# Encoder step: the background of the gated delta rule in another order

## The chip, the cores and the metric

The kernel runs on one core of one Trainium2 chip. A core has five engines that run side by side, each with its own instruction stream, taken strictly in order: TensorE (PE, matrix products; its weight loads are listed as PEld), VectorE (DVE), ScalarE (ACT), GpSimd (POOL) and SyncE (SP), which here issues the DMAs. The metric is the device time of one call in microseconds; the median of the runs is what counts.

## The reference, cut to what matters

One layer of a hybrid encoder is computed for 1024 prompt tokens and 32 sample tokens of width 1024. One large projection of the normalised input feeds four branches: A (short convolution), B (gated recurrence), C (a 31-tap convolution, then a layer norm) and D (gated delta rule with 8 heads). Their outputs are projected, gated, added, projected once more, and normalised. The parts that matter here are branch D, and the convolution of branch C:

```python
qkv, new_conv_d = causal_dwconv(col(OFF_D, 2 * W_QK + W_D), conv_d, p['d_conv_w'])   # 4 taps
qkv = jax.nn.silu(qkv.astype(f32))
decay = jnp.exp(jnp.where(incl, gc[..., :, None] - gc[..., None, :], -jnp.inf))
a_mat = jnp.where(strict, jnp.einsum('nbhid,nbhjd->nbhij', kb, k) * decay, 0.0)
t_mat = a_mat + jnp.eye(c, dtype=a_mat.dtype)
u_base = lax.linalg.triangular_solve(t_mat, v * beta[..., None], left_side=True, lower=True, unit_diagonal=True)
def step(s, xs):                      # one chunk of frames after the other
    u = u0 - jnp.einsum('bhcd,bhde->bhce', w_, s)
    o = jnp.einsum('bhcd,bhde->bhce', qd, s) + jnp.einsum('bhij,bhje->bhie', pm, u)
    s = s * ge[..., None, None] + jnp.einsum('bhcd,bhce->bhde', ke, u)
c_glu = col(OFF_C, W_C) * jax.nn.sigmoid(col(OFF_C + W_C, W_C))
c_cv, new_conv_c = causal_dwconv(c_glu, conv_c, p['c_conv_w'])                          # 31 taps
```

## The kernel before

**The foreground is a row of jobs on TensorE.** A job is one block of 128 output columns of the large projection: 8 blocks of the inner dimension, 3 chunks of 352 tokens, and three products for each (high part of the weights with the high and the low part of the input, low part of the weights `wl` with the high part of the input), so 72 products of 352 columns on L212. `run` loads the weights of the next job when a job begins: a DMA into `wr`, a cast on ACT into `wh` (L179) and a subtraction on DVE into `wl` (L181), called the split here. `wh` and `wl` have two buffers each, so the split of a job can start only when TensorE has done the job two before it. A job's first product with its own `wl` stands, as written, 16 products into the job.

After five jobs at the start, which share the reading of the input, `jobs` holds the jobs of the 8 heads (q, k and v, 20 jobs), then those of branches A and C in the order of the table `ORDER`: 54 jobs, numbered 0 to 53 here, and six more in `last`. Jobs that follow, in pairs, use fewer products and don't change.

**The background runs in queues.** After each third of a chunk a job calls `bg()`, nine times in a job, and `bg()` advances every queue by its rate: a rate of 3 divided by PARTS (3) is one step for each call. A step is the part of a generator between two `yield`s. The queues that matter: `qt` (short convolutions), `qa` (`gdn_a`, which for one head makes what the delta rule needs), `qu` (`base`, and later `base_s`), `qi` (`inverses`), `qs` (`states`), `qc` (the convolutions of branch C).

- `gdn_a(h)` works on three groups of chunks of 128 tokens: 4, 4, and the 32 sample tokens. First it transposes k and q of every group (L478), with sums of squares on ACT (L480) and the scaled k on DVE (L483). Then for each group it loads the running decay `Gb` from DRAM (L498), subtracts (DVE, L501), takes two exponentials on ACT and a mask on POOL, which makes `E` and `EU`, multiplies q (L507), transposes v (L511), forms k times k and k times q (L530, L541) and multiplies with `E` and `EU` (L521, L522). Everything is stored to DRAM through SP.
- `base` solves all triangular blocks of 64 by elimination: 63 columns, one product (L564, `bt`) and one subtraction (L565, `bx`) on DVE for each, of 63 to 1024 elements a partition; each instruction needs the one before it. `base_s` does the same for the sample tokens (31 columns, on 8 partitions, tiles `st` and `sx`).
- `inverses` and `states` then go over the chunks, in two groups of four heads: the first group's eight chunks, then the second's, then the sample tokens.
- The convolution of branch C is a chain of 29 DVE instructions (L315, `accc`) and two more for each of 8 blocks; three of the blocks are done in this stage and five in the next.

A scheduler that works with estimates of its own then places what was written on the engines; an instruction whose inputs are not ready in its reckoning is passed by others. So the order on an engine is not quite the written one, and it is fixed when the program is built.

Of the kernel before, what the change touches and what calls it, by code (L numbers as in the profile page):

```python
# [9 lines left out]
F32 = mybir.dt.float32  # L10
# [43 lines left out]
def encoder_step(ctx: ExitStack, tc: tile.TileContext, I, O):  # L54
# [395 lines left out]
    def gdn_a(h):  # L450
# [3 lines left out]
        for _ in range(3 if h == 0 else 0):  # L454
            yield
# [38 lines left out]
        for c0, n, L in groups:  # L494
            cr = slice(c0, c0 + n)
            Gb = gt("Gb")
            src = d_gc[c0 * 8 + h:c0 * 8 + h + 1, 0:L]
            sp.dma_start(Gb[:, :n, :L], bass.AP(tensor=src.tensor, offset=src.offset, ap=[[0, 128], [8 * 128, n], [1, L]]))  # L498
            E = gt("E", 1)
# [4 lines left out]
            EU = gt("EU")  # L504
# [3 lines left out]
            put("qd", Gb[:, :n, :L], c0, n, L)  # L508
            ps = aux()
# [57 lines left out]
    def base():  # L567

        a = POOL[-1].tile([128, 64, 64], F32, name="ba")
        x = POOL[-1].tile([128, 64, 64], F32, name="bx")  # L570
        tmp = POOL[-1].tile([128, 1024], F32, name="bt")
        sp.dma_start(a, d_ab.rearrange("p (i j) -> p i j", i=64))
        yield
        yield from eliminate(a, x, tmp, 64)
        sp.dma_start(d_x2.rearrange("p (i j) -> p i j", i=64), x[0:64])
        for r in range(0, 64, 16):
            act.copy(a[:, r:r + 16, :], x[:, :, r:r + 16].rearrange("p i j -> p j i"))
            yield
        sp.dma_start(d_yt.rearrange("p (i j) -> p i j", i=64), a)
        next_stage("gc")  # L580
        for hg in range(2):
            qi.items.append(inverses(hg))
            qs.items.append(states(hg, range(8)))
        qu.rate = 0.3 / PARTS
        qu.items.append(base_s())

    def base_s():

        a = POOL[-1].tile([128, 32, 32], F32, name="sa")[:8]
        x = POOL[-1].tile([128, 32, 32], F32, name="sx")[:8]  # L590
# [12 lines left out]
    def next_xy():  # L603
        nxy[0] += 1
        return XY[nxy[0] % 2]

    def load_g(name, hg, c, bufs, p=128, L=128):
        t = gt("l_" + name, bufs)
        sp.dma_start(t[:p, :, :L], d_g[name][hg * 9 + c, :p, :, :L])
        return t  # L610

    def inverses(hg):

        for c in range(8):
            while len(inv_t) >= 2:
                yield
# [33 lines left out]
    def states(hg, chunks):  # L650
# [4 lines left out]
        for c in chunks:  # L655
# [7 lines left out]
            if c == 8:  # L663
                S = gt("S", 2)
# [15 lines left out]
            U = gt("U")  # L680
# [6 lines left out]
            S2 = gt("S", 2)  # L687
# [13 lines left out]
            o = gt("o")  # L701
            f = gp.tile([128, 3, 4], F32, name="f")
# [14 lines left out]
            oT = gt("oT")  # L717
# [221 lines left out]
    for q in (qa, qu, qi, qs):  # L939
# [12 lines left out]
    qc.drain()  # L952
# [251 lines left out]
    qx.drain()  # L1204
    psum(6, 2)
# [260 lines left out]
```

## Time and profile before

| what | us |
|---|---|
| median of 3 runs (2254.4 to 2257.28) | 2256.55 |
| the profiled execution | 2259.44 |
| its span, from the first to the last instruction | 2257.7 |
| TensorE busy | 2198.2 (97%) |
| DVE busy | 1645.8 (73%) |
| ACT busy | 1006.8 (45%) |

The profiled execution is 0.13% longer than the median. A TensorE that is busy 97% of the span leaves 59.5 us in which it does nothing; times in which its clock is granted at half speed come on top. Where these lie is read from windows of the trace, from the waits of TensorE, and from the instructions in order of time.

### The profile page before, as it was taken

How to read it: one execution, taken by the hardware profiler on the slowest of the kernel's cores; microseconds unless marked ns; L12 is line 12 of the kernel's file. 1: busy time of each engine (PE TensorE's matmuls, PEld its weight loads, DVE VectorE, ACT ScalarE, POOL GpSimd, SP SyncE). 2: the span in 40 equal slices, each digit the busy share in tenths (PEclk: the TensorE clock that was granted, in tenths of full speed). 3: DMA queues.
4: the chain of work that ended last, by engine and by line, in shares of the span. 5: the costliest groups of instructions: out<-in, count | busy, mean ns of one | idle time of the engine just before them, and what ended most of it. 6: DMA issues, size and time to landing. Idle time of an engine off the chain costs nothing.

```text
span 2257.7 us, 38700 instructions
## 1 busy us (share of the span) xinstructions
PE 2198.2 (97%) x15334; PEld 2139.7 (95%) x15334; DVE 1645.8 (73%) x2668; ACT 1006.8 (45%) x1939; POOL 162.0 (7%) x257
## 2 busy tenths in 40 slices
PE   7999999999999999999999999999999999999998
PEld 7999989999999998999999999999999899999976
DVE  7586665599998634778969697966676679855565
ACT  4587876411133443333444444446666245522200
POOL 3121011100000000000000000000000000100043
PEclk9999999999999999999999999999999999999999
DMA  6154454421155564223333333333344898775422
GB/s 233 44 141 126 125 132 108 127 67 48 58 173 177 178 181 135 61 91 99 126 115 114 108 122 127 102 106 121 104 145 137 339 317 309 286 275 173 132 96 75
DMA packets 198160, 323.71 MB, mean 143 GB/s; under 512 B 52793, under 2 KB 117131, under 8 KB 197659
## 3 DMA queue, kind: packets, MB, share of 16 engines
q1 hardware_dynamic: 197979, 321.25, 44.2%
q8 instruction: 120, 1.97, 0.4%
q14 instruction: 61, 0.50, 0.1%
HBM read 211.12 MB, written 110.06 MB: 142 GB/s over the span
## 4 chain that ended last, share of the span: by engine, by line
PE 70%; DVE 9%; DMA 3%; issue 2%; ACT 1%; SPq 0%; DVEq 0%; ACTq 0%
PE mm L1066 31%; PE mm L212 26%; PE mm L1391 4%; PE mm L224 2%; DVE accc L315 2%; DVE bt L564 1%; PE aux L1173 1%; DVE bx L565 1%; DMA Gb<-d_gc 1%; PE aux L679 1%; PE aux L686 1%; DVE yl L1327 1%; PE aux L699 1%; PE aux L698 1%; PE aux L670 1%
## 5 line engine op out<-in xcount | busy, mean ns | idle before, releaser
L315 DVE SCALAR_TENSOR_TENSOR accc<-padc,cols,accc 128x1086 f32<-128x1086 f32 (+2 forms) x250 | 335.1, 1341 | 10.8 <-ACT accc L312 9.4
L212 PE MATMUL mm<-xh,wh 128*128 128x352 f32 (+2 forms) x1600 | 299.4, 325 | 2.7 <-ACT xh L876 0.9
L212 PE MATMUL mm<-xl,wh 128*128 128x352 f32 (+2 forms) x1600 | 301.2, 325 | 0.0
L212 PE MATMUL mm<-xh,wl 128*128 128x352 f32 (+2 forms) x1568 | 295.0, 327 | 3.6 <-DVE wl L181 3.6
L212 PEld LDWEIGHTS mm<-xh,wh 128*128 128x128 f32 x1600 | 259.2, 190 | 5.0 <-DVE padc L737 1.3
L212 PEld LDWEIGHTS mm<-xh,wl 128*128 128x128 f32 x1568 | 257.9, 192 | 5.4 <-DVE wl L181 3.9
L212 PEld LDWEIGHTS mm<-xl,wh 128*128 128x128 f32 x1600 | 259.1, 190 | 1.9 <-issue 0.4
L1066 PE MATMUL mm<-xh,o 128*128 128x264 f32 x1152 | 217.1, 284 | 0.0
L179 ACT CAST wh<-wr 128x1024 fp32r<-128x1024 f32 x96 | 100.7, 1049 | 254.9 <-PE mm L212 212.2
L1066 PEld LDWEIGHTS mm<-xh,o 128*128 128x128 f32 x1152 | 181.3, 188 | 0.0
L1066 PE MATMUL mm<-xl,o 128*128 128x264 f32 x576 | 163.7, 284 | 0.0
L1078 ACT COPY mu<-mm 128x264 f32<-128x264 f32 x216 | 81.0, 377 | 148.2 <-PE mm L1066 146.3
L181 DVE TENSOR_TENSOR wl<-wr,wh 128x1024 fp32r<-128x1024 f32 x96 | 116.8, 1217 | 36.2 <-ACT wh L179 14.7
L1084 DVE TENSOR_TENSOR ev<-mm,mu 128x264 f32<-128x264 f32 x216 | 91.2, 426 | 30.9 <-ACT mu L1078 16.0
L1066 PE MATMUL mm<-xh,wh 128*128 128x264 f32 x576 | 112.3, 285 | 1.1 <-ACT xh L1124 1.1
L1030 ACT CAST o<-wr 128x512 fp32r<-128x512 f32 x108 | 66.8, 619 | 102.4 <-PE mm L1066 86.5
L1066 PE MATMUL mm<-th,o 128*128 128x264 f32 x576 | 112.0, 285 | 0.2
L1066 PE MATMUL mm<-th,wh 128*128 128x264 f32 x576 | 111.8, 285 | 0.0
L1066 PE MATMUL mm<-th,wl 128*128 128x264 f32 x576 | 111.2, 284 | 0.0
L1066 PE MATMUL mm<-xh,wl 128*128 128x264 f32 x576 | 110.6, 284 | 0.0
L1066 PEld LDWEIGHTS mm<-xl,o 128*128 128x128 f32 x576 | 108.2, 188 | 0.0
L212 PE MATMUL mm<-yh,wh 128*128 128x352 f32 x552 | 100.8, 324 | 0.0
(335 smaller groups left out, 4864.9 us busy)
## 6 DMA issues: line engine op xcount, KB each, us to landing
wr<-in_w_in SPq DMA_DIRECT2D x137, 512.0 KB, 3.7
d_z<-ev SPq DMA_DIRECT2D x64, 264.0 KB, 2.2
d_gate<-ev SPq DMA_DIRECT2D x64, 264.0 KB, 2.1
st<-d_t SPq DMA_DIRECT2D x32, 528.0 KB, 6.2
st<-d_z SPq DMA_DIRECT2D x32, 528.0 KB, 8.0
wr<-in_w_branch SPq DMA_DIRECT2D x32, 512.0 KB, 4.4
ev<-d_gate SPq DMA_DIRECT2D x30, 528.0 KB, 5.7
d_mix<-ev SPq DMA_DIRECT2D x24, 528.0 KB, 4.7
```

The costliest lines, as they stand in the source:

```text
L179: act.copy(hi, raw)
L181: dve.tensor_sub(lo, raw, hi.bitcast(F32))
L212: pe.matmul(ps[:, :c[1]], lhsT=w[:, k, :], rhs=r(k)[:, cs(c)], start=(n == 0), stop=(n == len(todo) - 1))
L224: pe.matmul(ps[:, :c[1]], lhsT=w[:, k, :], rhs=r(k)[:, cs(c)], start=(n == 0), stop=(n == len(todo) - 1))
L315: dve.scalar_tensor_tensor(acc, pad[:, i:i + W], col(name, ci, i), acc, op0=OP.mult, op1=OP.add)
L564: dve.tensor_tensor(tv, a[:, j + 1:, j:j + 1].to_broadcast([P, n, m]), x[:, j:j + 1, 0:m].to_broadcast([P, n, m]), op=OP.mult)
L565: dve.tensor_tensor(x[:, j + 1:, 0:m], x[:, j + 1:, 0:m], tv, op=OP.subtract)
L1030: act.copy(t[:, 0:4], src)
L1066: pe.matmul(b, lhsT=w[:, wo + k, :], rhs=XS[name](p, k)[:, sl], start=(start and n == 0), stop=(stop and n == 11), skip_group_check=True)
L1078: act.copy(mu[name][:, c * HC:(c + 1) * HC], b)
L1084: dve.tensor_add(res[i][:, a:a + HC], b, mu[name][:, c * HC:(c + 1) * HC])
L1391: pe.matmul(ps, lhsT=a[k][:, ts], rhs=w[k][:, hs], start=(n == 0), stop=(n == len(todo) - 1))
```

## The change

In `gdn_a` the decay matrices of a group are made one group ahead: the loads of `Gb` for the first two groups stand before the loop and that for the third within it, `Gb`, `E` and `EU` get two buffers, and `decay` for the next group is written ahead of the products of the present one. Every head now waits three steps at its start, and there are three more `yield`s in the loop; the rate of `qa` goes from 3 to 2.6. One block of branch C (`c_jobs(0)`, two jobs and its convolution) is put behind the jobs of head 2; in `ORDER` the other blocks of C go behind those of A. `base_s` gets a queue of its own and runs beside `base`, not behind the states. `inverses` takes the two groups of heads in turn, `states` runs in two queues, one for each group, with tiles of its own, and the rates change. The last wait for the convolutions (`qc.drain`) moves behind the jobs of `last`. No arithmetic is changed, and SP, DVE, PE and POOL have as many instructions as before; ACT has seven table loads more.

```diff
-        for _ in range(3 if h == 0 else 0):
+        for _ in range(3):
             yield
...
-        for c0, n, L in groups:
-            cr = slice(c0, c0 + n)
-            Gb = gt("Gb")
+
+        def load_decay(c0, n, L):
+            Gb = gt("Gb", 2)
             src = d_gc[c0 * 8 + h:c0 * 8 + h + 1, 0:L]
             sp.dma_start(Gb[:, :n, :L], bass.AP(tensor=src.tensor, offset=src.offset, ap=[[0, 128], [8 * 128, n], [1, L]]))
-            E = gt("E", 1)
+            return Gb
+
+        def decay(Gb, c0, n, L):
+            E, EU = gt("E", 2), gt("EU", 2)
...
+        Gbs = {0: load_decay(*groups[0]), 1: load_decay(*groups[1])}
+        EE = {0: decay(Gbs[0], *groups[0])}
+        yield
+        for gi, (c0, n, L) in enumerate(groups):
+            cr = slice(c0, c0 + n)
+            E, EU = EE[gi]
+            if gi + 1 < 3:
+                EE[gi + 1] = decay(Gbs[gi + 1], *groups[gi + 1])
+                if gi == 0:
+                    Gbs[2] = load_decay(*groups[2])
+                yield
...
         if h == 7:
+            qc.rate = 0.4 / PARTS
             next_stage("gb")
             qu.items.append(base())
+            qu2.items.append(base_s())
...
+        qu2.drain()
         next_stage("gc")
+        qi.items += [inverses(), inverses_s()]
         for hg in range(2):
-            qi.items.append(inverses(hg))
-            qs.items.append(states(hg, range(8)))
-        qu.rate = 0.3 / PARTS
-        qu.items.append(base_s())
+            qs[hg].items += [states(hg, range(8)), states(hg, [8])]
+        qc.rate = 1.9 / PARTS
...
-        for c in range(8):
-            while len(inv_t) >= 2:
+    def inverses():
+
+        for c, hg in [(c, hg) for c in range(8) for hg in range(2)]:
+            while len(inv_t) >= len(XY):
...
-    qi = queue("inv", 1.9)
-    qs = queue("state", 1.9, 0.67)
-    qa = queue("gdn_a", 3)
+    qi = queue("inv", 2.0)
+    qs = [queue("state0", 1.2), queue("state1", 1.2, 0.5)]
+    qa = queue("gdn_a", 2.6)
     qu = queue("base", 1.7)
+    qu2 = queue("base_s", 0.5)
     qt = queue("short", 2)
-    qc = queue("conv", 1.1)
-    ORDER = "A0 A1 X0 C0 X1 A2 C1 X2 A3 C2 X3 A4 C3 X4 A5 C4 X5 C5 C6 C7"
+    qc = queue("conv", 1.0)
+    ORDER = "A0 A1 X0 A2 X1 A3 X2 A4 X3 A5 X4 C1 X5 C2 C3 C4 C5 C6 C7"
...
+        if h == 2:
+            jobs += c_jobs(0)
...
     qt.drain()
-    qc.drain()
     p1c.close()
...
     qx.drain()
+    qc.drain()
```

What this does to the order on the engines, at the three places that matter (line numbers differ between the two programs):

SP, around the decay loads of the fourth head, before: the load of `Gb` for the first group, the store `d_qd` of what is made from it, and the next load.

```order
L498 DMA Gb<-d_gc 128x4x128
L466 DMA d_pt<-st 32x32
L466 DMA d_ke<-st 128x4x128
L466 DMA d_k<-ev 128x4x128 x2
L466 DMA d_k<-ev 128x32
L466 DMA d_ke<-st 128x4x128
L466 DMA d_qd<-Gb 128x4x128
L177 DMA wr<-in_w_in 128x1024
L498 DMA Gb<-d_gc 128x4x128
```

SP, the fourth head after (its first load of `Gb`, and the stores of the head before it):

```order
L498 DMA Gb<-d_gc 128x4x128
L466 DMA d_r<-st 128x4x128
L549 DMA d_a<-st 64x4x64
L553 DMA d_ab<-st 64x4x64 x2
L466 DMA d_pt<-st 128x4x128
L466 DMA d_qd<-Gb 128x32
L466 DMA d_r<-st 128x4x128
L549 DMA d_a<-st 64x4x64
L553 DMA d_ab<-st 64x4x64 x2
L177 DMA wr<-in_w_in 128x1024
L466 DMA d_pt<-st 128x4x128
L466 DMA d_r<-st 32x128
```

The load now stands ahead of the last stores (`d_r`, `d_a`, `d_ab`, `d_pt`) of the head before, in which its `d_qd` is not reached; before, `d_qd` stood six rows behind it.

DVE, from the split of job 34 to the split of job 35, in the middle of the elimination, before:

```order
L181 TENSOR_TENSOR wl<-wr,wh 128x1024
L565 TENSOR_TENSOR bx<-bx,bt 128x23x41
L315 SCALAR_TENSOR_TENSOR accc<-padc,cols,accc 128x1086
L564 TENSOR_TENSOR bt<-ba,bx 128x924
L315 SCALAR_TENSOR_TENSOR accc<-padc,cols,accc 128x1086
L565 TENSOR_TENSOR bx<-bx,bt 128x22x42
L315 SCALAR_TENSOR_TENSOR accc<-padc,cols,accc 128x1086
L564 TENSOR_TENSOR bt<-ba,bx 128x903
L315 SCALAR_TENSOR_TENSOR accc<-padc,cols,accc 128x1086
L565 TENSOR_TENSOR bx<-bx,bt 128x21x43
L181 TENSOR_TENSOR wl<-wr,wh 128x1024
```

DVE, from the split of job 34 on, after (12 of the 21 instructions that stand before the split of job 35):

```order
L181 TENSOR_TENSOR wl<-wr,wh 128x1024
L582 TENSOR_TENSOR bt<-ba,bx 128x999
L582 TENSOR_TENSOR st<-sa,sx 8x207
L583 TENSOR_TENSOR bx<-bx,bt 128x27x37
L583 TENSOR_TENSOR sx<-sx,st 8x9x23
L582 TENSOR_TENSOR bt<-ba,bx 128x988
L582 TENSOR_TENSOR st<-sa,sx 8x192
L583 TENSOR_TENSOR bx<-bx,bt 128x26x38
L583 TENSOR_TENSOR sx<-sx,st 8x8x24
L582 TENSOR_TENSOR bt<-ba,bx 128x975
L582 TENSOR_TENSOR st<-sa,sx 8x175
L583 TENSOR_TENSOR bx<-bx,bt 128x25x39
```

The convolution is gone from between the two eliminations' instructions; `base` and `base_s` alternate, and more of them stand between two splits.

PE, where the products with `wl` (here `xh,wl`) of one job stand latest, before (job 36):

```order
L212 MATMUL mm<-xh,wh 128x352 x8
L212 MATMUL mm<-xl,wh 128x352 x8
L212 MATMUL mm<-xh,wh 128x352 x8
L212 MATMUL mm<-xl,wh 128x352 x8
L212 MATMUL mm<-xh,wh 128x352 x8
L212 MATMUL mm<-xl,wh 128x352 x8
L212 MATMUL mm<-xh,wl 128x352 x24
```

PE, the same after (job 34, and the first of job 35 ahead of the products with `wl` of job 34):

```order
L212 MATMUL mm<-xh,wh 128x352 x8
L212 MATMUL mm<-xl,wh 128x352 x8
L212 MATMUL mm<-xh,wh 128x352 x8
L212 MATMUL mm<-xl,wh 128x352 x8
L212 MATMUL mm<-xh,wh 128x352 x8
L212 MATMUL mm<-xl,wh 128x352 x8
L212 MATMUL mm<-xh,wh 128x352 x8
L212 MATMUL mm<-xl,wh 128x352 x8
L212 MATMUL mm<-xh,wh 128x352 x7
L212 MATMUL mm<-xh,wl 128x352 x24
```

The products with `wl` are placed behind all others of the job in both, after it also behind 23 products of the next job.

## Rows read from the trace of the kernel before

**Rows 1.** The page's first part: busy time, share of the span and number of instructions of TensorE.

```profile
PE 2198.2 (97%) x15334; PEld 2139.7 (95%) x15334; DVE 1645.8 (73%) x2668; ACT 1006.8 (45%) x1939; POOL 162.0 (7%) x257
```

**Rows 2.** Windows of the trace: the stretch (us), its length, busy us and number of instructions of PE, PEld, DVE, ACT and POOL, then the mean granted clock of TensorE (1 is full speed), the share of the DMA engines and GB/s. The three stretches are the heads, the elimination, and the inverses and states.

```profile
80.00:430.00 350.00, 333.11 (x2133) 322.06 (x2132) 238.93 (x487) 261.11 (x606) 45.97 (x118) 0.98 0.44 118
430.00:640.00 210.00, 205.56 (x1256) 204.75 (x1255) 199.02 (x236) 42.15 (x46) 13.65 (x17) 0.98 0.23 72
640.00:960.00 320.00, 315.46 (x2226) 295.51 (x2225) 205.85 (x431) 132.42 (x319) 8.98 (x15) 0.99 0.51 153
```

**Rows 3.** Waits of TensorE from 80 to 430 us: who waited for whom, us in total, times, the longest.

```profile
PE aux L478 <- DVE st L483: 7.5, 4, 3.0
PE aux L541 <- DVE st L522: 5.0, 2, 4.4
PE aux L478 <- ACT junk L480: 2.2, 2, 1.8
```

**Rows 4.** Windows (columns as in rows 2) right behind the longer waits of TensorE, three among the heads and one in the elimination.

```profile
194.00:205.00 11.00, 7.95 (x44) 7.42 (x43) 6.57 (x9) 8.35 (x25) 1.01 (x3) 0.84 0.44 121
286.00:300.00 14.00, 9.61 (x46) 9.38 (x45) 11.02 (x18) 10.28 (x15) 2.65 (x5) 0.76 0.46 130
354.00:366.00 12.00, 9.60 (x53) 8.88 (x52) 4.68 (x7) 10.58 (x35) 1.59 (x3) 0.86 0.33 103
594.00:606.00 12.00, 7.56 (x32) 6.82 (x31) 12.00 (x17) 1.29 (x1) 0.12 (x1) 0.72 0.27 90
```

**Rows 5.** DVE in order of time, just ahead of three of the waits of rows 3: start, us, the instruction, and in brackets how long DVE had waited and for what.

```profile
191.63 0.88 DVE L501 TENSOR_SCALAR E<-Gb,gc 128x128 f32<-128x128 f32 x4 [3.27 <-DMA Gb<-d_gc]
...
285.22 0.87 DVE L501 TENSOR_SCALAR E<-Gb,gc 128x128 f32<-128x128 f32 x4 [2.88 <-DMA Gb<-d_gc]
...
350.78 0.68 DVE L501 TENSOR_SCALAR E<-Gb,gc 128x128 f32<-128x128 f32 x3 [5.82 <-DMA Gb<-d_gc]
```

**Rows 6.** The tile `Gb`: time from the issue of its DMAs to their landing.

```profile
DMA to landing us min/median/max: 2.3/4.2/6.1
```

**Rows 7.** TensorE in order of time, in the elimination: jobs 29, 37 and 38 begin at 496.24, 589.38 and 608.19.

```profile
496.24 1.46 PE L212 MATMUL mm<-xh,wh 128*128 128x352 f32 x8
...
498.83 1.46 PE L212 MATMUL mm<-xh,wl 128*128 128x352 f32 x8
...
589.38 1.46 PE L212 MATMUL mm<-xh,wh 128*128 128x352 f32 x8
...
598.29 5.06 PE L212 MATMUL mm<-xh,wl 128*128 128x352 f32 x16 [3.57 <-DVE wl L181]
...
608.19 1.46 PE L212 MATMUL mm<-xh,wh 128*128 128x352 f32 x8
...
612.88 0.32 PE L212 MATMUL mm<-xh,wl 128*128 128x352 f32 x1
```

**Rows 8.** Groups of DVE instructions from 430 to 640 us: line, tiles, shape, number | busy us, mean ns of one | idle us before them.

```profile
L315 DVE SCALAR_TENSOR_TENSOR accc<-padc,cols,accc 128x1086 f32<-128x1086 f32 x42 | 56.4, 1342 | 0.0
L565 DVE TENSOR_TENSOR bx<-bx,bt 128x63 f32<-128x63 f32 (+31 forms) x63 | 55.2, 876 | 0.4
L564 DVE TENSOR_TENSOR bt<-ba,bx 128x63 f32<-128x63 f32 (+31 forms) x63 | 55.1, 874 | 0.5
L181 DVE TENSOR_TENSOR wl<-wr,wh 128x1024 fp32r<-128x1024 f32 x17 | 20.7, 1217 | 0.0
L811 DVE TENSOR_TENSOR pad<-mm,ev 128x352 f32<-128x352 f32 (+2 forms) x16 | 6.6, 424 | 8.3 <-PE mm L212 8.3
L825 DVE TENSOR_TENSOR ev<-mm,ev 128x352 f32<-128x352 f32 x12 | 6.2, 516 | 0.0
...
L318 DVE SCALAR_TENSOR_TENSOR ev<-pad,cols,acc 128x1024 f32<-128x1024 f32 (+1 forms) x6 | 4.6, 761 | 0.0
```

**Rows 9.** DVE in order of time, from the split of job 29 on, and the split of job 38.

```profile
487.20 1.22 DVE L181 TENSOR_TENSOR wl<-wr,wh 128x1024 fp32r<-128x1024 f32 x1
488.33 1.15 DVE L564 TENSOR_TENSOR bt<-ba,bx 128x960 f32<-128x960 f32 x1
489.40 1.34 DVE L315 SCALAR_TENSOR_TENSOR accc<-padc,cols,accc 128x1086 f32<-128x1086 f32 x1
490.67 1.15 DVE L565 TENSOR_TENSOR bx<-bx,bt 128x960 f32<-128x960 f32 x1
491.74 1.34 DVE L315 SCALAR_TENSOR_TENSOR accc<-padc,cols,accc 128x1086 f32<-128x1086 f32 x1
...
611.19 1.22 DVE L181 TENSOR_TENSOR wl<-wr,wh 128x1024 fp32r<-128x1024 f32 x1
```

**Rows 10.** DVE in order of time, the first instruction of the elimination and the last of its first 28 (63 and 700 elements).

```profile
441.38 0.26 DVE L564 TENSOR_TENSOR bt<-ba,bx 128x63 f32<-128x63 f32 x1
...
460.90 0.89 DVE L565 TENSOR_TENSOR bx<-bx,bt 128x700 f32<-128x700 f32 x1
```

**Rows 11.** Groups as in rows 8, from 640 to 760 us, the elimination of the sample tokens.

```profile
L564 DVE TENSOR_TENSOR st<-sa,sx 8x31 f32<-8x31 f32 (+15 forms) x31 | 9.9, 320 | 0.0
L565 DVE TENSOR_TENSOR sx<-sx,st 8x31 f32<-8x31 f32 (+15 forms) x31 | 9.9, 320 | 0.0
```

**Rows 12.** Waits of TensorE from 640 to 960 us.

```profile
PE aux L716 <- DVE o L711: 2.2, 1, 2.2
PE aux L635 <- DVE st_c L769: 1.8, 1, 1.8
```

More of the change, by code (lines that the diff above doesn't have):

```diff
@@ L508, in gdn_a @@
             put("qd", Gb[:, :n, :L], c0, n, L)
+            return E, EU
+        Gbs = {0: load_decay(*groups[0]), 1: load_decay(*groups[1])}
[9 more added lines that the diff above has]
+                yield
             ps = aux()
@@ L592, in base_s @@
         sp.dma_start(a, d_abs.rearrange("p (i j) -> p i j", i=32))
+        yield
+        yield
         yield from eliminate(a, x, tmp, 32)
@@ L595, in base_s @@
         sp.dma_start(d_yts.rearrange("p (i j) -> p i j", i=32), a)
-        qi.items.append(inverses_s())
-        qs.items.append(states(0, [8]))
-        qs.items.append(states(1, [8]))
     XY = []
@@ L604, in next_xy @@
         nxy[0] += 1
-        return XY[nxy[0] % 2]
+        return XY[nxy[0] % len(XY)]
     def load_g(name, hg, c, bufs, p=128, L=128):
-        t = gt("l_" + name, bufs)
+        t = gt(f"l_{name}{hg}", bufs)
         sp.dma_start(t[:p, :, :L], d_g[name][hg * 9 + c, :p, :, :L])
         return t
-    def inverses(hg):
-        for c in range(8):
-            while len(inv_t) >= 2:
+    def inverses():
+        for c, hg in [(c, hg) for c in range(8) for hg in range(2)]:
+            while len(inv_t) >= len(XY):
                 yield
@@ L641, in inverses_s @@
         for hg in range(2):
-            while len(inv_t) >= 2:
+            while len(inv_t) >= len(XY):
                 yield
@@ L663, in states @@
             if c == 8:
-                S = gt("S", 2)
+                S = gt(f"S{hg}", 2)
                 sp.dma_start(S, I["delta"][hs].rearrange("h p n -> p h n"))
@@ L679, in states @@
                 pe.matmul(ps[:L, h, :], lhsT=Y[:L, h, :L], rhs=R[:L, h, :], start=True, stop=True)
-            U = gt("U")
+            U = gt(f"U{hg}")
             act.copy(U[:L], ps[:L])
@@ L686, in states @@
                 pe.matmul(ps[:, h, :], lhsT=ke[:L, h, :], rhs=U[:L, h, :], start=True, stop=True)
-            S2 = gt("S", 2)
+            S2 = gt(f"S{hg}", 2)
             if S is not None:
@@ L700, in states @@
             S = S2
-            o = gt("o")
-            f = gp.tile([128, 3, 4], F32, name="f")
+            o = gt(f"o{hg}")
+            f = gp.tile([128, 3, 4], F32, name=f"f{hg}")
             act.copy(o[:L], ps[:L])
@@ L716, in states @@
                 pe.transpose(ps[:, h, :L], o[:L, h, :], ident[:L, :L])
-            oT = gt("oT")
+            oT = gt(f"oT{hg}")
             act.activation(oT[:, :, :L], ps[:, :, :L], AF.Copy, scale=col("d_g", 0))
@@ L938, in encoder_step @@
     run(jobs, last[0])
-    for q in (qa, qu, qi, qs):
+    for q in (qa, qu, qi, *qs):
         while q.items:
```

1 line of the change is left out of this document (removed).

## The prediction

> **What bounds the kernel now.** I read the busy times first. TensorE is busy for 2198.2 us of the span [rows 1], so the work of TensorE sets the time, and a change of order can only win or lose what TensorE doesn't do in its gaps, and what its clock doesn't give. The change touches the first stage alone: from the jobs of `last` on, TensorE's order is the same in both programs. The second view is therefore the windows of that stage [rows 2]: among the heads (80 to 430 us) TensorE is idle for 350 - 333.1 = 16.9 us, in the elimination (430 to 640) for 210 - 205.6 = 4.4 us, in the inverses and states (640 to 960) for 320 - 315.5 = 4.5 us. DVE is busy for 68% of the first stretch, 95% of the second and 64% of the third: it is DVE that TensorE can come to wait for.
>
> The third view is who TensorE waited for [rows 3]. Among the heads 12.5 us in 6 waits end with DVE's `st`, the scaled k and the masked product; 2.2 us end with ACT. Right behind the longer of these waits the granted clock is at half speed (1.2 GHz) for a part of the windows [rows 4]; at half speed a stretch loses half, so a mean of 0.84 over 11 us is 1.8 us lost, 0.76 over 14 us 3.4, 0.86 over 12 us 1.7: 6.8 us. The fourth view goes to DVE ahead of these waits [rows 5]: it stands still, not for want of work, but in front of `E<-Gb`, until the load of the decay has landed (3.3, 2.9 and 5.8 us). What is queued behind on DVE, convolutions and the `st` that TensorE wants, stands with it. A load takes 4.2 us in the median, up to 6.1 [rows 6].
>
> In the elimination TensorE waits once in earnest, for a split: job 37 takes from 589.38 to 608.19, 18.8 us, where the eight jobs before take 93.14 / 8 = 11.64 us each [rows 7].
>
> **The heads.** `Gb` is loaded ahead of the stores of the head before, its use comes later by a half to two jobs, 6 us and more, where it was mostly a fifth of a job: more than the longest landing. So the waits with that root go. I leave 1.2 us of the 12.5 for the two shortest waits, which I can't trace to `Gb`: 11.3 us of waits and 6.8 us of clock are 18.1 us won. What is late next: the convolution of C0 is now here, 31 instructions of 1.34 us [rows 8], 41.5 us, and with two splits and the evictions of its two jobs DVE has 239 + 46 = 285 us in 350 + 23 - 18 = 355 us, 80% where it had 68%. That hides as long as no `st` comes late; the bound on this side is that half the gain goes, 9 us. More than all, 12.5 + 2.2 + 6.8 = 21.5 us, can't be won. The three to six further steps for a head issue nothing, and SP has the same DMAs. One wait is new: the third load of `Gb` stands on SP until the store of the first group has read its buffer; behind it on SP is the next job's weight load, which has the better part of a job, over 10 us, to spare. POOL makes the masks earlier and is busy for 46 of the 350 us; its work stays hidden. The seven more table loads on ACT, about 1.3 us each, are 9 us beside an ACT that is three quarters busy here at most; uncovered they would cost those 9.
>
> **The elimination.** Here I count what DVE must do from the split of job 29 to the split of job 37, in the new order: 93 of the 126 instructions of `base`, 63 of `base_s`, 38 others. First a check of the method on the kernel before [rows 7, 9]. From the split of job 29 (487.20) to that of job 38 (611.19) DVE takes 124.0 us, and the nine jobs would take TensorE 9 x 11.64 = 104.8: DVE falls back by 19.2 us. How far it may fall: the split of job 29 is done at 488.42, the first product with its `wl` stands at 498.83, 10.4 us spare; in job 38 that product stands 4.69 us into the job, not 2.59, which makes 12.5. So TensorE should wait 6.7 us; job 37 took 7.2 us more than its 11.64. The method holds.
>
> Now the change. `base`: 63 `bt` and 63 `bx` take 110.3 us [rows 8], less the 33 small ones at both ends, from 0.26 to 0.89 us [rows 10], on the mean of these 28 x 0.58 + 5 x 0.29 = 17.7: 92.6 us. `base_s`: 31 + 31 of 0.32 us [rows 11] and a copy of about 1.1: 20.9. The others [rows 8]: 8 splits of 1.217, 12 `pad` of 0.424, 9 `ev` of 0.516, 6 ends of a convolution of 0.761, 3 taps of 1.34: 28.0 us. Together 141.5 us in 194 instructions. An instruction that doesn't need its neighbour starts ahead of the neighbour's end: 488.33 + 1.15 is 489.48, and the next starts at 489.40; four in a row give 0.08 us each [rows 9]. `base` and `base_s` alternate now, so I take that for all 194: 141.5 - 15.5 = 126.0 us. Eight jobs are 93.1 us for TensorE: DVE falls back by 32.9. Spare: DVE has little to do in job 28, so the split of job 29 starts when its buffer is free, at the start of job 28, is done 1.22 us later and wanted 11.64 + 2.59 us later, 13.0 us; in job 37 the product with `wl` stands 28 products in, not 16, at 0.162 us each 1.9 more: 15.0. TensorE waits 32.9 - 15.0 = 17.9 us. The order agrees: only at the products with `wl` of jobs 33 and 35 do rows of elimination stand on DVE with no product beside them. Half speed comes behind it: before, 12 x 0.28 = 3.4 us [rows 4]; while DVE sets the pace most of it hides in the next wait, so I take 2.5, and 20.4 us in all. Before it was 4.4 + 3.4 = 7.8: 12.6 us lost.
>
> Here a rule speaks against the change more than the row does. By the row an independent instruction starts 0.08 us ahead of its neighbour's recorded end. The Trainium skill, page "VectorE: DVE Perf Modes", section "The DRAIN you can't avoid", says that the next DVE instruction does not start until the pipe of the one before has emptied. By that the elimination's demand would be the full 141.5 us; the trace does not agree, and I go by the row. It returns below as a rival.
>
> **Inverses and states.** Before, 4.5 us idle and, at a clock of 0.99 over 320 us, 3.2 us of half speed: 7.7 [rows 2]. The two waits of substance are for a forced end of a convolution (`st_c`) and for an `o` that stood behind the sample elimination on DVE [rows 12]. `base_s` has left this stretch, and the two groups of heads alternate, which puts other products between the steps of one chain. The trace shows no such interleaving; bounds are 0 and twice the 7.7, and I take 5.0, near the row: 2.7 us won.
>
> **The sum.** -18.1 + 12.6 - 2.7 = -8.2 us against the profiled execution's 2259.4: 2251.2. The median of the runs is 2.9 us below that execution, so 2248.3 us.
>
> **The rivals.**
> - The elimination waits more, and the kernel is slower: if instructions of `base` and `base_s` that alternate don't overlap, DVE needs 141.5 us, falls back by 48.4, and TensorE waits 33.4, 15.5 us more: 2263.8. It decides from a wait of 17.9 + 12.8 = 30.7 us on. For it: each needs the one two places before; against it: [rows 9] shows overlap in just such a pattern, with a convolution in the place of `base_s`. Chance 0.10. By the sentence of the Trainium skill above (VectorE: DVE Perf Modes) this would be the rule.
> - The heads keep half of their waits, since DVE, 80% busy, has the `st` late again: 9 us won, not 18.1: 2257.4, within 0.2%. For it: the convolution's long instructions stand between the short ones; against it: DVE need not stand still any more. Chance 0.19.
> - The elimination waits no more than before, because DVE gets to the first column earlier or later than I think and has more to spare: 12.6 less, 2235.7. Against it: the order on DVE is fixed. Chance 0.13.
> - The two chains of states stand in each other's way: 15.4 us of waits there, not 5.0: 2258.7. Chance 0.06.
> - The loads of `Gb` don't come early enough, the change doesn't do what it says: nothing won among the heads, 2266.4. The order on SP speaks against it. Chance 0.02.
>
> **How the numbers follow.** The forecast, 2248.3, has 0.50, with a spread of its own from 2241 to 2254. A measurement of this kernel can tell about 0.2% (4.5 us) from no change, so faster means under 2252.0 and slower over 2261.1. Of the forecast 0.47 is faster and 0.03 the same; the elimination without more waits adds 0.13 to faster; the kept half of the heads' waits 0.18 to the same and 0.01 to faster; the chains of states 0.05 to the same and 0.01 to slower; the longer elimination and the missing effect 0.12 to slower. Faster 0.61, same 0.26, slower 0.13. The range from 2236 to 2261 leaves out the slow rivals and the lower half of the early elimination, less than 0.2.
>
> **What would show it.** Right: no wait of DVE for `Gb` over 1 us past the first head, and waits of TensorE for `st` under 2 us among the heads; two groups of waits of TensorE for the split `wl` in jobs 33 to 36, 15 to 20 us together, with rows of `bt`, `st`, `bx`, `sx` on DVE beside them and half speed behind; no new wait of over 2 us among inverses and states. Wrong: waits for `st` as before among the heads with DVE busy at their side; waits for `wl` under 10 or over 30 us; a time of the later stages that differs from before by over 2 us.

## The result, and the profile after

| | before | after |
|---|---|---|
| median of 4 runs each, us | 2255.59 (2254.4 to 2257.28) | 2243.35 (2242.49 to 2243.96) |
| ratio, 95% interval | 1 | 0.9945 (0.9929 to 0.9960) |
| span of the profiled execution, us | 2257.7 | 2241.8 |

The change wins 12.2 us by the medians; 8.2 were forecast, and 2248.3 us. The profiled execution of before, at 2259.4 us, lay 3.9 us above this median, so the two spans differ by more, 15.9 us. TensorE's part of the page, then the windows of the three stretches as in [rows 2]:

```profile
PE 2185.6 (97%) x15334; PEld 2133.3 (95%) x15334; DVE 1649.1 (74%) x2668; ACT 1014.3 (45%) x1946; POOL 171.1 (8%) x257
```

```profile
80.00:430.00 350.00, 339.67 (x2208) 330.80 (x2207) 274.60 (x505) 255.77 (x592) 58.12 (x118) 1.00 0.44 117
430.00:640.00 210.00, 195.32 (x1185) 194.24 (x1185) 171.91 (x283) 44.51 (x62) 14.01 (x21) 0.95 0.27 84
640.00:960.00 320.00, 320.00 (x2298) 304.21 (x2297) 205.75 (x373) 147.17 (x333) 3.49 (x11) 1.00 0.50 149
```

Against [rows 2]: among the heads TensorE is idle for 10.3 us, not 16.9; in the elimination for 14.7, not 4.4, at a clock of 0.95; among inverses and states not at all, where 4.5 us were idle.

Windows are fixed in time, while the work shifts. For the comparison of kernels I therefore take TensorE's products from start to start, each against the median of its form, and add up what is over the median. That holds waits, half speed and the small gaps where one kind of product follows another. **Lost** means this sum, in us, of one profiled execution: heads from job 0 to the first `bt`; elimination to 20 us behind the last `bx`; states to job 54; last from there to the first products of job 60, behind the pairs, some 860 us of which the six jobs of `last` are the first 70; rest behind it.

| kernel | heads | elimination | states | last | rest | median, us | ratio |
|---|---|---|---|---|---|---|---|
| before | 39.1 | 10.0 | 33.2 | 23.7 | 11.9 | 2255.6 | 1 |
| after | 27.9 | 22.8 | 19.6 | 22.2 | 8.7 | 2243.4 | 0.9945 |
| after less before | -11.2 | +12.8 | -13.6 | -1.5 | -3.2 | | |

The start adds 0.3 us; the sum is -16.4, for 15.9 us of span. From job 54 on TensorE's products stand in the same order in both kernels and in runs 1, 2, 4, 6, 8, 9, 11 and 12 below. Last and rest together lose between 30.2 and 33.1 us in all of these but the execution of before, which loses 35.6: the -4.7 there is no effect that can be told from the spread of single executions.

Who TensorE waits for among the heads, as in [rows 3], and DVE's waits for the load there, before and after:

```profile
PE aux L478 <- DVE st L483: 3.4, 5, 1.6
PE aux L478 <- ACT junk L480: 3.3, 2, 2.5
PE aux L546 <- DVE st L538: 3.3, 2, 2.5
PE aux L557 <- DVE st L538: 0.3, 1, 0.3
```

```profile
DVE E L501 <- DMA Gb<-d_gc: 30.6, 13, 5.8
```

```profile
DVE E L504 <- DMA Gb<-d_gc: 2.6, 1, 2.6
```

The waits of [rows 5] are gone: one is left, in the first head, where 30.6 us in 13 waits were. But 10.3 us of TensorE's waits remain, some with other roots. At 180 us DVE waits not for `Gb` but for the buffer of its own output `st`, whose store `d_r` is not done reading it, and TensorE waits behind it; at 251 us ACT is late with the squares: it had itself stood 2.5 us for DVE (`ev`), and a table load and exponentials stand between the squares:

```profile
177.20 0.23 DVE L504 TENSOR_SCALAR E<-Gb,gc 32x32 f32<-32x32 f32 x1
180.20 0.76 DVE L538 TENSOR_TENSOR st<-aux,EU 128x256 f32<-128x256 f32 x2 [2.77 <-DMA d_r<-st]
```

```profile
247.03 1.09 ACT L428 ACTIVATE ev<-ev 128x1056 f32<-128x1056 f32 x1 [2.52 <-DVE ev L318]
...
249.27 1.28 ACT L506 ACT_TABLE_LOAD   x1
250.56 0.63 ACT L506 ACTIVATE E<-E 128x512 f32<-128x512 f32 x1
251.10 0.26 ACT L480 ACTIVATE junk<-aux 128x128 bf16<-128x128 f32 x1
```

In the elimination TensorE waits twice, at the products with `wl` of jobs 33 and 35, the two jobs that the order had named; half speed follows. The waits in order of time, and windows around them as in [rows 4]:

```profile
543.73 5.06 PE L212 MATMUL mm<-xh,wl 128*128 128x352 f32 x16 [7.09 <-DVE wl L181]
...
577.46 5.06 PE L212 MATMUL mm<-xh,wl 128*128 128x352 f32 x16 [7.58 <-DVE wl L181]
```

```profile
536.00:550.00 14.00, 6.91 (x27) 6.62 (x26) 14.00 (x17) 0.90 (x2) 0.00 (x0) 0.63 0.13 37
569.00:584.00 15.00, 7.42 (x29) 7.12 (x28) 15.00 (x25) 0.00 (x0) 0.00 (x0) 0.66 0.11 35
```

DVE has work in every microsecond of both windows. Jobs 33 and 35 take 21.60 and 22.27 us in place of 11.64: 20.6 us, of which 14.7 are the two waits and 5.7 products at half speed. DVE itself, as in [rows 9], the split of job 29, a piece of the elimination and the split of job 37:

```profile
474.53 1.22 DVE L181 TENSOR_TENSOR wl<-wr,wh 128x1024 fp32r<-128x1024 f32 x1
...
499.18 0.94 DVE L582 TENSOR_TENSOR bt<-ba,bx 128x768 f32<-128x768 f32 x1
500.05 0.34 DVE L582 TENSOR_TENSOR st<-sa,sx 8x192 f32<-8x192 f32 x1
500.32 0.94 DVE L583 TENSOR_TENSOR bx<-bx,bt 128x768 f32<-128x768 f32 x1
...
600.94 1.23 DVE L181 TENSOR_TENSOR wl<-wr,wh 128x1024 fp32r<-128x1024 f32 x1
```

From split to split it is 126.4 us, for 194 instructions whose durations add up to 140.6. 499.18 + 0.94 is 500.12, and the independent next step starts at 500.05.

### The profile page after: what moved, and what is told of

Its sections match the earlier page's. It is cut to its first block, busy times and chain, and to the rows that moved or that the text cites. A ratio compares the mean times of both kernels' runs of the same rounds, so it can differ in the third digit from the quotient of the medians.

```text
span 2241.8 us, 38629 instructions
## 1 busy us (share of the span) xinstructions
PE 2185.6 (97%) x15334; PEld 2133.3 (95%) x15334; DVE 1649.1 (74%) x2668; ACT 1014.3 (45%) x1946; POOL 171.1 (8%) x257
## 4 chain that ended last, share of the span: by engine, by line
PE 73%; DVE 9%; ACT 2%; issue 2%; DMA 2%; SPq 0%; DVEq 0%; ACTq 0%
PE mm L1085 32%; PE mm L212 27%; PE mm L1411 4%; PE mm L224 2%; DVE bt L582 2%; DVE bx L583 2%; PE aux L1192 1%; PE aux L703 1%; DVE yl L1347 1%; PE aux L716 1%; PE aux L696 1%; DVE wl L181 1%; PE aux L715 1%; PE aux L687 1%; DVE st L1315 1%
## 5 line engine op out<-in xcount | busy, mean ns | idle before, releaser
L212 PE MATMUL mm<-xh,wl 128*128 128x352 f32 (+2 forms) x1568 | 289.6, 327 | 14.7 <-DVE wl L181 14.7
L212 PE MATMUL mm<-xh,wh 128*128 128x352 f32 (+2 forms) x1600 | 293.4, 324 | 1.8 <-ACT xh L894 0.9
L212 PE MATMUL mm<-xl,wh 128*128 128x352 f32 (+2 forms) x1600 | 292.1, 323 | 0.0
L212 PEld LDWEIGHTS mm<-xh,wl 128*128 128x128 f32 x1568 | 255.3, 192 | 16.7 <-DVE wl L181 15.3
L1050 DVE TENSOR_TENSOR o<-wr,o 128x512 fp32r<-128x512 f32 x108 | 74.0, 688 | 36.4 <-ACT o L1049 36.1
```

What stands on the lines that cost most here:

```text
L212: pe.matmul(ps[:, :c[1]], lhsT=w[:, k, :], rhs=r(k)[:, cs(c)], start=(n == 0), stop=(n == len(todo) - 1))
L1050: dve.tensor_sub(t[:, 4:8], src, t[:, 0:4].bitcast(F32))
```

## The experiments

Twelve kernels, each timed in five rounds against the kernel before. The "lost" columns of all of them, with the medians and ratios:

| kernel | heads | elimination | states | last | rest | median, us | ratio (95% interval) |
|---|---|---|---|---|---|---|---|
| 1 base_s on POOL | 26.4 | 25.6 | 23.4 | 23.7 | 8.7 | 2248.7 | 0.9974 (0.9963 to 0.9984) |
| 2 decays alone | 20.0 | 18.7 | 28.8 | 24.1 | 9.0 | 2242.1 | 0.9947 (0.9934 to 0.9961) |
| 3 one chain | 26.3 | 20.8 | 18.7 | 27.3 | 8.4 | 2246.4 | 0.9960 (0.9947 to 0.9972) |
| 4 C0 back | 21.6 | 25.1 | 25.6 | 22.4 | 9.4 | 2246.3 | 0.9961 (0.9949 to 0.9974) |
| 5 one chain, base_s behind base | 26.6 | 2.3 | 19.9 | 29.0 | 8.6 | 2227.9 | 0.9881 (0.9868 to 0.9895) |
| 6 base slower | 27.3 | 7.8 | 24.7 | 22.4 | 7.8 | 2231.4 | 0.9897 (0.9882 to 0.9913) |
| 7 decays alone, base slower | 22.9 | 19.2 | 22.8 | 25.9 | 10.1 | 2242.5 | 0.9948 (0.9934 to 0.9961) |
| 8 loads alone | 20.8 | 12.0 | 28.6 | 24.4 | 7.3 | 2237.0 | 0.9922 (0.9909 to 0.9934) |
| 9 two chains, base_s behind base | 26.5 | 2.7 | 22.2 | 22.5 | 9.2 | 2224.8 | 0.9871 (0.9858 to 0.9885) |
| 10 as 5, states faster | 28.4 | 2.3 | 26.2 | 24.7 | 8.0 | 2231.0 | 0.9898 (0.9884 to 0.9912) |
| 11 as 10, loads alone | 21.9 | 2.4 | 27.0 | 23.1 | 8.6 | 2224.3 | 0.9871 (0.9858 to 0.9885) |
| 12 as 9, loads alone | 21.7 | 2.6 | 21.5 | 22.6 | 8.1 | 2217.4 | 0.9829 (0.9813 to 0.9845) |

**1. The sample elimination on POOL.**

```diff
-        yield from eliminate(a, x, tmp, 32)
+        yield from eliminate(a, x, tmp, 32, pool)
```

> The changed kernel, with the 62 steps of the sample elimination (base_s) on POOL in place of DVE. Theory A (DVE's total work between the splits of jobs 29 and 37 sets the wait of TensorE): DVE has 141.5 - 20.9 = 120.6 us left there, in which the steps of base follow each other directly, so that little of it overlaps; 120.6 less 93.1 is 27.5, less a spare of 15 is a wait of 12.5 us in place of the 20.6 measured, so 8 us less: 2235 us, and jobs 33 to 36 together longer than 46.6 us by 12 instead of 20. Rival B (the order in which rows of base and base_s are bunched between two splits makes the wait, not their sum): the wait stays between 18 and 22 us, 2243. Rival C (POOL at work slows DVE): steps of base longer than their 0.87 us on the mean, wait over 22 us, slower than 2244.

Slower than the changed kernel, and with longer steps of `base` (0.92 us on the mean for 0.87), as rival C had it; but its waits of over 22 us did not come. TensorE waits 12.9 us for splits, and jobs 32 to 34 take 15.3 us too long, less than the 20.6 of the changed kernel. Most of those 12.9 are a wait that none of the three had named: the copy `sa<-sx` behind the sample elimination stayed on DVE, and DVE stood in front of it until POOL was through; `base` and the splits stood behind it, and TensorE waited 10.78 us for a split. What makes the kernel slower is another wait, 6.9 us for a load of the first inverse (`l_a`) with half speed behind it, some 10 us of the 25.6; why that load comes late was not tried. Beside that DVE and POOL slow each other: a split that takes 1.21 takes 1.66 us.

```profile
PE mm L212 <- DVE wl L181: 12.9, 3, 10.8
PE aux L646 <- DMA l_a<-d_a: 6.9, 1, 6.9
```

```profile
504.34 1.66 DVE L181 TENSOR_TENSOR wl<-wr,wh 128x1024 fp32r<-128x1024 f32 x1
505.92 1.43 DVE L583 TENSOR_TENSOR bx<-bx,bt 128x768 f32<-128x768 f32 x1
521.69 1.02 DVE L614 COPY sa<-sx 8x1024 f32<-8x1024 f32 x1 [14.33 <-POOL sx L583]
```

It tells nothing about theory A; run 5 does.

**2. The decays a group ahead, and nothing else, in the kernel before.** The edit is the part of the change in `gdn_a`, at the old rate of 3.

> The kernel before with one part of the change: the decay matrices a group ahead (two buffers each of Gb, E and EU, three steps more per head and two between the groups), at the old rate of 3. Theory A (what the heads did not win, 11.7 of the forecast 18.1 us, is due to the convolution of C0 among them): without that convolution the heads win 16 to 18 us, elimination and states as before: 2238 to 2240 us. Rival B (the rest comes with the new order itself: waits of DVE for a buffer of st whose store has not been read, and ACT late): the heads win 9 to 12 us: 2244 to 2247 us, and the waits of DVE for the stores of st (7.0 us after) are there.

Among the heads theory A holds: 39.1 lost become 20.0, 19.1 us won where the whole change wins 11.2. The time is 2 us longer than theory A had it, since the elimination loses 8.7 us more: in job 37 TensorE waits for a split and then for `padc` on DVE, behind the forced end of C0's convolution.

```profile
80.00:430.00 350.00, 345.47 (x2254) 336.22 (x2253) 250.24 (x508) 260.14 (x608) 54.98 (x122) 1.00 0.46 127
```

```profile
578.40 4.23 PE L212 MATMUL mm<-xh,wl 128*128 128x352 f32 x15 [3.86 <-DVE wl L181]
592.08 2.13 PE L212 MATMUL mm<-xh,wh 128*128 128x352 f32 x6 [8.26 <-DVE padc L752]
```

This one part alone is as fast as the whole change.

**3. One chain of states again.**

```diff
-        for c, hg in [(c, hg) for c in range(8) for hg in range(2)]:
+        for c, hg in [(c, hg) for hg in range(2) for c in range(8)]:
...
-            qs[hg].items += [states(hg, range(8)), states(hg, [8])]
+            qs[0].items.append(states(hg, range(8)))
...
-    qi = queue("inv", 2.0)
-    qs = [queue("state0", 1.2), queue("state1", 1.2, 0.5)]
+    qi = queue("inv", 1.9)
+    qs = [queue("state0", 1.9, 0.67), queue("state1", 1.2, 0.5)]
```

> The changed kernel with inverses and states of the two groups of heads one after the other again, as before (one queue of states at rate 1.9), base_s still beside base. Theory A (the 13.5 us that TensorE lost less among inverses and states come from the two chains side by side): 10 to 13 us are given back there, 2253 to 2256 us, with a wait of 0.2 to 0.3 us at nearly each product of a chain. Rival B (they come from base_s having left that stretch and from the convolutions' new rate): at most 4 us are given back, 2243 to 2247 us.

Rival B: 3.0 us given back, in the states that slid behind job 54 (27.3 lost in place of 22.2, and 6.2 for 2.0 in the six jobs of `last` alone). In the states' own stretch one chain loses as little as two. So theory A, that two chains side by side are the gain there, falls.

**4. C0 back among the A and X jobs.**

```diff
-        if h == 2:
-            jobs += c_jobs(0)
...
-    ORDER = "A0 A1 X0 A2 X1 A3 X2 A4 X3 A5 X4 C1 X5 C2 C3 C4 C5 C6 C7"
+    ORDER = "A0 A1 X0 C0 A2 X1 A3 X2 A4 X3 A5 X4 C1 X5 C2 C3 C4 C5 C6 C7"
```

> The changed kernel with the two jobs of C0 and its convolution back between X0 and A2, no convolution among the heads. Read by stretches. Theory A (C0's convolution keeps the heads' waits up): what TensorE loses among the heads falls from 12 to 5 to 7 us; the convolution's 41 us now stand in the elimination and behind it, which costs 10 us or more there: 2243 to 2255 us. Rival B (the heads' remaining waits have another root): heads lose 10 to 13 us as in the changed kernel.

Theory A: the heads lose 21.6 in place of 27.9 (5.1 us idle in the windows, not 10.3), and the convolution costs 2.3 in the elimination and 6.0 among the states instead. Of TensorE's waits those at L478 for DVE stay; those for the products with the masks (L538) fall from 3.6 to 0.4 us, those for ACT's squares from 3.3 to 0.2.

```profile
80.00:430.00 350.00, 344.93 (x2243) 334.97 (x2242) 244.19 (x480) 257.12 (x605) 48.00 (x121) 1.00 0.44 117
```

```profile
PE aux L478 <- DVE st L483: 4.0, 5, 1.6
PE aux L557 <- DVE st L538: 0.4, 1, 0.4
PE aux L478 <- ACT junk L480: 0.2, 1, 0.2
```

**5. The sample elimination behind `base`,** as in the kernel before, in the kernel of run 3; the two groups of heads share their tiles again.

```diff
         if h == 7:
             qu.items.append(base())
-            qu2.items.append(base_s())
...
-        qu2.drain()
         next_stage("gc")
+        qu2.items.append(base_s())
```

> The one-chain variant of the changed kernel with the sample elimination (base_s) behind base again, as in the kernel before, on DVE; decays ahead and C0 among the heads stay. Theory A (the sum of DVE's work between the splits of jobs 29 and 37 sets the wait): without base_s 120.6 us of work are left, TensorE waits 8 to 13 us there in place of 20, while inverses and states lose up to 5 us more to base_s: 2238 to 2243 us. Rival B (base alone is too dense, base_s only filled the pipe's gaps between its dependent steps): the wait stays at 17 us or more, 2246 or slower.

More than theory A: no wait of TensorE is left in the elimination, every job from 28 to 41 takes 11.6 us, and 18.5 us are won against run 3. Counted in the two traces, DVE takes 97.0 us from the split of job 29 to that of job 37, not 126.4: the steps of `base_s` are gone, and of `base` 74 stand there in place of 93, since the last comes a job later. That second part theory A had not counted: with all 93 in place it left 8 to 13 us of wait. The states with `base_s` among them lose 1.2 us more, last 1.7.

```profile
430.00:640.00 210.00, 210.00 (x1317) 209.35 (x1315) 175.16 (x236) 46.78 (x57) 14.84 (x21) 1.00 0.31 96
```

**6. `base` slower, `base_s` beside it** (1.4 in place of 1.7; states 1.4, inverses 2.3).

> The changed kernel with base at a rate of 1.4 in place of 1.7 (and states 1.4, inverses 2.3, so that they end no later). Theory A (sum of DVE's work per job): 18% fewer steps of base per job are some 16 us less between the splits of jobs 29 and 37, so the wait falls from 20.6 us to below 8: 2231 to 2236 us, if the states, which begin two to three jobs later and are denser, lose no more than 20 us as in the changed kernel. Rival B (steps are bunched by the order, whatever the rate): two waits of 7 us or more stay, 2241 or slower. Rival C (denser states stand in each other's way): the wait goes, states lose over 28 us.

Theory A: jobs 35 and 36 take 14.6 and 14.0, 5.3 us too long together in place of 20.6, DVE 113.5 us from split to split (79 steps of `base`). 5 of the 15 us come back in the denser states, which lose 24.7, more than the 20 that it allowed.

```profile
PE mm L212 <- DVE pad L828: 2.1, 3, 1.4
PE mm L212 <- DVE wl L181: 1.9, 2, 1.6
```

**7. The decays alone, `base` slower.**

```diff
-    qu = queue("base", 1.7)
+    qu = queue("base", 1.5)
```

> The kernel before with the decay matrices a group ahead, and base at a rate of 1.5 in place of 1.7. With the decays alone TensorE waited 17 us at the split of job 37. Theory A: 12% fewer steps per job are 11 us less work for DVE in the eight jobs before, the wait falls to 4 to 8 us: 2229 to 2235 us. Rival B (the wait is made by what DVE does in that one job, an end of a convolution and nineteen steps in a row): it stays over 12 us, 2239 or slower.

Job 37 takes 29.2 us as before (28.7 in run 2): rival B by the numbers. But the edit did not reach what it was meant to change: on DVE the rows of the elimination stand in the same order as in run 2, step for step. So it tells nothing on theory A. The heads stand in the same order too and lose 22.9 in place of 20.0: so far apart do two executions of one order lie.

**8. Only the loads of `Gb` ahead, in the kernel before,** with two buffers for `Gb`; `load_decay` holds the load as it was.

```diff
         for c0, n, L in groups:
+            if c0 == 4:
+                load_decay(*groups[0])
+                load_decay(*groups[1])
             put("k", tv(kT, c0, n, L), c0, n, L)
...
-            Gb = gt("Gb")
-            src = d_gc[c0 * 8 + h:c0 * 8 + h + 1, 0:L]
-            sp.dma_start(Gb[:, :n, :L], ...)
+            Gb = Gbs[c0]
...
             put("qd", Gb[:, :n, :L], c0, n, L)
+            if c0 == 0:
+                load_decay(*groups[2])
```

> The kernel before with only the loads of Gb ahead (two buffers; the first two loads of a head among its first transposes, the third behind the first group's use), decays computed where they were, no further steps. Theory A (the landing of Gb, for which DVE stood 30.6 us in 13 waits, is the root of the heads' waits): DVE's waits for Gb fall below 6 us and the heads win 12 to 19 us, but the elimination gives up to 9 back as with the decays alone: 2237 to 2246 us. Rival B (the root is the dense chain of decays itself on DVE, ACT and POOL, and the further steps that spread it): the waits for Gb go, but become waits for ACT's exponentials at the same place, the heads win under 7 us, 2248 or slower.

Theory A: DVE's waits for `Gb` fall from 30.6 to 5.2 us and the heads win 18.3. Neither the decays a group ahead nor the further steps are needed for it, and the elimination gives back 2.0, not 8.7.

```profile
80.00:430.00 350.00, 344.71 (x2250) 335.38 (x2249) 249.89 (x511) 258.06 (x608) 56.60 (x124) 1.00 0.46 127
```

```profile
DVE E L509 <- DMA Gb<-d_gc: 5.2, 3, 2.5
```

**9. Two chains, the sample elimination behind `base`:** the changed kernel with the edit of run 5; the two groups of heads share `U`, `o` and `oT`.

> The changed kernel with both chains side by side and the sample elimination behind base (so that it fits, the two heads' groups share one buffer each of U, o and oT). It isolates base_s in the states. Theory A (the gain among inverses and states is a sum: C0's convolution out 6, chains side by side 4, base_s out 3 to 5 us): the elimination loses 2 to 3 us, states and the jobs of last lose 3 to 5 us more than in the changed kernel: 2223 to 2228 us. Rival B (base_s among two chains stands in their way, since their steps are nearer together): over 10 us more lost, 2232 or slower. Rival C (base_s costs nothing there): 2220 to 2223 us.

Theory A: 2224.8. Elimination 2.7, states and `last` together 44.7 where the changed kernel has 41.8: `base_s` costs 2.9 there, and its leaving the elimination gives 20.1.

```profile
430.00:640.00 210.00, 210.00 (x1318) 209.00 (x1317) 174.96 (x236) 47.17 (x58) 14.85 (x21) 1.00 0.31 97
```

**10. Run 5 with states and inverses at 2.2 in place of 1.9.**

> The one-chain variant with base_s behind base (2227.9 us), states and inverses at rates of 2.2 in place of 1.9. Theory A (that variant still lost 5 us because 12 us of the states' work had slid behind the last of the numbered jobs, where it stands less covered): the jobs of last lose 22 to 24 us again in place of 29: 2221 to 2225 us. Rival B (denser states wait as much as they save): 2226 to 2231 us.

Rival B: last loses 24.7, near the 22 to 24 of theory A, but the states lose 26.2 in place of 19.9: 3.1 us slower.

**11. Run 10 with the heads of run 8** (rate 3, loads alone ahead; C0 among the heads).

> The kernel of the run before this one, with the heads of the run in which only the loads of Gb were ahead (no further steps, rate 3, decays where they are used), C0 still among the heads. Theory A (the loads are the whole gain among the heads; the decays a group ahead add nothing): the heads lose 25 to 29 us, as in the changed kernel, and the time is within 3 us of the run before this one. Rival B (with C0's convolution on DVE the room of a step between decay and use is needed): the heads lose over 32 us, 5 us or more slower.

Neither: 6.8 us faster. The heads lose 21.9, though C0's convolution is there as in the changed kernel (29 instructions of 1.35 us in the window) and DVE waits 9.2 us for `Gb`, 5.2 in run 8.

```profile
80.00:430.00 350.00, 344.23 (x2250) 334.67 (x2249) 281.93 (x531) 268.06 (x613) 59.43 (x117) 1.00 0.46 122
```

**12. Runs 9 and 11 together:** two chains, `base_s` behind `base`, C0 and the loads alone among the heads.

> All that the runs speak for together: chains side by side, C0 among the heads and the sample elimination behind base (the run of 2224.8 us), with only the loads of Gb ahead among the heads (rate 3). Theory A (the parts add up: the heads lose 22 us as with the loads alone and C0 there, not 26.5; elimination 2 to 3; states and the jobs of last 44 to 46): 2218 to 2222 us. Rival B (the heads end two jobs earlier, so the stretch behind shifts against the other jobs, and the states give back what the heads win): 2223 to 2228 us.

Theory A, 0.6 us below its range: the parts add up. This is the fastest of all, 38 us below the kernel before and 26 below the changed one.

```profile
PE 2178.8 (98%) x15334; PEld 2127.3 (96%) x15334; DVE 1651.1 (74%) x2668; ACT 1017.1 (46%) x1948; POOL 176.2 (8%) x257
```

```profile
80.00:430.00 350.00, 344.24 (x2257) 335.23 (x2255) 281.10 (x528) 267.94 (x614) 59.15 (x118) 1.00 0.46 121
430.00:640.00 210.00, 210.00 (x1339) 207.79 (x1338) 168.68 (x228) 51.26 (x77) 14.84 (x22) 1.00 0.32 103
640.00:960.00 320.00, 319.00 (x2247) 304.04 (x2245) 218.27 (x424) 136.78 (x308) 7.70 (x13) 1.00 0.45 135
```

## Why the prediction was right, and where two steps were not

**The elimination: right, by its mechanism and its size.** 126.0 us of work for DVE from split to split were forecast, 126.4 are there; waits in jobs 33 and 35 of 20.4 us with the half speed, 20.6 came; 12.6 us lost, 12.8 came. The parts of the 20.4 were not those that came: 17.9 us of waits and 2.5 of half speed were forecast, 14.7 and 5.7 measured, and 14.7 is just under the 15 to 20 us named as the sign. Behind the first wait half speed took the place of further waiting; DVE sets the sum, and the sum holds. Runs 5 and 6 show that DVE's work between the splits makes the wait: with 97.0 us of it no wait is left, and for the 113.5 of run 6 the prediction's own sum gives 113.5 - 93.1 - 15.0 = 5.4 us, where 5.3 came. Run 5 also shows that moving `base_s` is enough to end it; but `base` thins out with that move, from 93 steps to 74, so what the steps of `base_s` cost by themselves is not shown. The rival that alternating steps don't overlap is out: they do, by 0.07 to 0.08 us, as in [rows 9]. The prediction's rule against it was half a rule: the section of the Trainium skill that it cites ("VectorE: DVE Perf Modes", "The DRAIN you can't avoid") goes on that a next instruction that is not held starts earlier. The trace agrees with that.

**The heads: the root right, the sum too high.** 18.1 us were forecast, 11.2 came, and of the waits for `st`, which were to be under 2 us, 7.0 are left. That the landing of `Gb` is the root is shown by run 8: its loads alone, moved ahead, win 18.3. The step that failed is "that hides as long as no `st` comes late; the bound on this side is that half the gain goes": C0's convolution does not hide beside the new decays, and takes 6.3 us (run 4), within the bound of 9 that made the second rival. But that rival's reason, the long instructions between the short ones, is only half of it: with the loads alone the heads lose 20.8 without the convolution (run 8) and 21.9 and 21.7 with it (runs 11 and 12), and with the decays ahead but no convolution 20.0, 22.9 and 21.6 (runs 2, 7 and 4). Only both together cost more than the 2.9 us by which runs 2 and 7, of one order there, differ (26.3 to 28.4 in the changed kernel and in runs 1, 3, 5, 6, 9 and 10). Run 4 shows where it is paid: in the waits for the products with the masks and for ACT's squares. Which part of the decays does it (the buffers of `st` that wait for their stores, as at 180 us, ACT's exponentials among the squares, as at 251 us, or 24 steps at 2.6 for 18 at 3) was not tried apart and stays open. The buffers' waits alone don't decide it: DVE waits 12.5 us for stores of `st` among the heads of the changed kernel, and 24.6 in run 2, which loses least. The seven more table loads, which the prediction set beside the heads, are not there: 47 stand among the heads, 49 before.

**Inverses and states: the direction right, the term far too small.** 2.7 us were forecast, 13.6 came, which made up for the heads. The term let 5.0 of 7.7 us of waits and half speed stay, "near the row"; none stayed, its lower bound. And it counted nothing but waits: of the 33.2 us lost there before only 9.1 were waits and half speed; the other 24.0 are gaps of under 0.2 us from start to start, 11.3 of them where unlike products meet. They fell to 19.6 (7.9 where unlike products meet), while the products of the chains now come in 74 runs, not 99. 9.1 and 4.4 are the 13.6 but for rounding. Which part of the change did this is shown only in part. Counted to the end of the six jobs of `last`, where the kernel before loses 1.6 us more and the changed one 2.0, 13.2 us were won. The reason given first, the two groups side by side, is worth 3.3 us of them (run 3); `base_s` out is worth 2.6 (run 9), C0's convolution out 5.6 (run 4). These make 11.5. Each is the difference of two single executions, good to about 3 us, so only the last is clear of that.

**The later stage: nothing, as forecast.** The stretch from job 54 on took 1333.7 us before and 1329.4 after, over the 2 us that the prediction had named as a sign against it. But runs 2 and 8, with before's kernel from there on, took 1331.5 and 1330.2, and the order on TensorE is the same in all four. The 4.3 us are mostly what one execution differs from the next by.

**Together:** -11.2 + 12.8 - 13.6 = -12.0, against -12.2 between the medians; the profiled execution of before lost some 4 us more behind job 54 than the others, and lay 3.9 us above its median. The forecast of -8.2 was near partly by luck: by two errors of opposite sign, 6.9 us too much for the heads and 10.9 too little for the states.

## What to carry to other kernels

Where an in-order engine stands in front of a load, move the load alone and look first: here that single move (run 8) won 17.0 us, the change of which it is a part 12.2. Two pieces of work on one engine should lie where the engine behind them has room: moving the 21 us of `base_s` out from beside `base`, where DVE was full, gave 20 us, `base` thinning out with it, and cost some 3 among the states, where DVE was 64% busy [rows 2]. And in a stretch of short chains count the gaps between unlike products too, not the waits alone.

## What was not expected of the hardware

DVE and POOL slow each other here. In run 1 the split takes 1.66 us beside POOL and 1.22 without; POOL's own 207-element step takes 0.85 us while DVE works and 0.54 when DVE stands. DVE's `ev<-mm,ev`, which reads one of its inputs from `mm` in PSUM, keeps its 0.51 us:

```profile
481.38 0.85 POOL L582 TENSOR_TENSOR st<-sa,sx 8x207 f32<-8x207 f32 x1
...
512.80 0.54 POOL L582 TENSOR_TENSOR st<-sa,sx 8x207 f32<-8x207 f32 x1
```

```profile
490.42 1.65 DVE L181 TENSOR_TENSOR wl<-wr,wh 128x1024 fp32r<-128x1024 f32 x1
...
493.23 0.51 DVE L842 TENSOR_TENSOR ev<-mm,ev 128x352 f32<-128x352 f32 x1
...
529.94 1.22 DVE L181 TENSOR_TENSOR wl<-wr,wh 128x1024 fp32r<-128x1024 f32 x1
```

The Trainium skill, page "GPSIMD Engine Reference", section "Key points", says that POOL shares its SBUF interfaces with VectorE and contends with instructions that have two SBUF inputs; these rows agree.
